# One decoder layer: the sample rows' high and low parts in one stationary tile, 512-wide value and memory products, memory transposes behind task 2, spare transposes in the opening

## The chip, the cores and the metric

The kernel is one program on one core of a Trainium2 chip. The metric is the time of one execution in microseconds of the device, as the median of several runs. TensorE (PE) multiplies: it holds a stationary tile of up to 128 x 128 and streams the columns of a second operand past it, into a bank of PSUM of 512 fp32 columns per partition. VectorE (DVE), ScalarE (ACT) and GpSimd (POOL) do the elementwise work, SyncE (SP) issues the transfers from HBM.

## What is computed

The reference is one inference step of one decoder layer in fp32, for 512 prompt tokens and 64 sample tokens (8 sequences of 8) that share all weights:

```python
h = rmsnorm(x, norm_pre_mix)                       # 1024 channels
ca, cb, hq, hf, hi, hgate, mq, gl = split(h @ w_in)
c     = silu(layernorm(causal_dwconv(ca * sigmoid(cb), conv_w)))   # width 31
p_conv = c @ w_conv_out
o     = hgrn2(silu(hq), hf, v=hi, state)           # 4 heads, chunks of 32
p_hg  = (rmsnorm(o) * silu(hgate)) @ w_hg_out
mk, mv = split(rmsnorm(mem_prompt) @ w_mem_kv)     # 256 memory tokens; sample: cached
p_mem = softmax(mq @ mk.T / sqrt(128)) @ mv @ w_mem_out
g     = sigmoid(gl)                                # three gates of 1024 channels
x     = x + rmsnorm((g0*p_conv + g1*p_hg + g2*p_mem) @ w_out)
x     = x + rmsnorm((silu(h2 @ w_gate) * (h2 @ w_up)) @ w_down)    # h2 = rmsnorm(x)
```

Outputs are both groups' `x`, the last convolution inputs, the recurrent states, and the prompt's memory keys and values.

## The kernel before

**Exactness.** Each fp32 operand of a large product is split into a high part in PE's fast fp32r format and a low part, the remainder (`split`, L99: ACT writes the high part, DVE the low one). A product is three matmuls: high x high, low x high, high x low (`mm3`, L94, and the same written out where the tokens are the stationary operand).

**Tokens.** The 576 tokens form five tiles (`TOK`, L37): four of 128 prompt tokens, and a fifth that begins at token 448, of which only the rows from 64 on, the 64 sample tokens, are used. Where channels are the output rows, tokens are streamed in two groups of 256 and 320 columns (`GRP`, L35). Where tokens are the output rows, a tile of 128 tokens is stationary and the weights are streamed: so in `v_cols` (L688, the recurrence's values), in `mem_kv` (L505, the memory's keys and values, two tiles of 128 memory tokens) and in `mix_out` (L1090, the product with `w_out`). The fifth tile so multiplies 64 prompt rows a second time and throws them away.

**Weights.** `wprep` (L110) loads a chunk of 1024 elements per partition into one of three raw buffers and splits it into one of three pairs of high and low buffers. `wplan` lists the chunks in the order of use, `wahead(n)` keeps n of them prepared (LOOK = 2, L895), `wnext` takes one. For `v_cols` and `mem_kv` a chunk has 512 rows of the weight and 256 columns; a task takes two chunks and does one half of the columns for all its token tiles: four memory tasks and two value tasks.

**Tasks and side work.** The list `tasks` (L1027 to 1057) holds four convolution input tasks (two weight chunks each), four memory tasks, two value tasks, four query tasks, then gates and recurrence heads, and the three branch outputs. Work for the other engines stands in generators that `pump` (L287) advances by a step after, and sometimes inside, each task: `convq` (the 31 taps on DVE, four taps to a step, and the tail), `side` (prompt attention, recurrence) and `sampq` (the sample's attention, `attn_sample`, L590). The order of each engine is then fixed by a scheduler that works from estimated times, with program order as priority; `tc.issue_after(ins)` puts what follows behind an instruction of the same engine.

**The memory rows.** After task 1, `mem_norm` (L494) loads the two tiles of memory tokens, takes their sums of squares on ACT, a reciprocal root on POOL, scales on DVE (L242), transposes on PE in four banks (L250) and splits (L105, L106). It is tied to task 1's last gate on ACT.

**The opening.** Fourteen matmuls of the identity (`WARM`, L184) run while the first tokens load. Then `norm_group` (L236) scales and transposes tiles 0 and 1, and, from `group_b` (L1012), tiles 2 to 4, the sample tile last.

**The sample's memory values.** `attn_sample` loads the cached values in eight units of 512 KB, one unit ahead of the matmuls that use it (L627 to 634).

**Output of the mixer.** `mix_out` takes the tiles in the order 4, 2, 3, 0, 1, each in two halves of 512 columns, 24 matmuls each; `ffn_norm` of a tile follows one tile later, and the feed-forward part begins with the group of tiles 2, 3 and 4. The x pool (`xtile`, L70) has five buffers, which hold the five tiles' residual rows there.

Of the kernel before, what the change touches and what calls it, by code (L numbers as in the profile page):

```python
# [42 lines left out]
def tile_decoder_layer(  # L43
# [17 lines left out]
    seq = [0]  # L61
# [32 lines left out]
    def mm3(out, whi, wlo, xhi, xlo, start, stop, more=False):  # L94
        T.matmul(out, lhsT=whi, rhs=xhi, start=start, stop=False, skip_group_check=more)  # L95
        T.matmul(out, lhsT=whi, rhs=xlo, start=False, stop=False, skip_group_check=more)  # L96
        T.matmul(out, lhsT=wlo, rhs=xhi, start=False, stop=stop, skip_group_check=more)  # L97
# [35 lines left out]
    last = {}  # L133

    def rsqrt(src, n, scale, p0=0, eng=None, eps=None):
# [20 lines left out]
        return y  # L156

# [78 lines left out]
    def norm_group(tiles, g0, hi, lo, c0, n, junk=None, eng=None):  # L236

        for xt, p0 in tiles:  # L240
            r = norm_rows(xt, p0, junk, eng)
            last["scale"] = V.tensor_scalar(xt[p0:, :], xt[p0:, :], r, None, op0=ALU.mult)  # L242
        per, ins = 512 // n, []
        for k0 in range(0, 8, per):
            ps = sdb()
            for kk in range(per):
                o = kk * n
                for xt, p0 in tiles:
                    m = P - p0
                    T.transpose(ps[:, o:o + m], xt[p0:, (k0 + kk) * P:(k0 + kk + 1) * P], ident[p0:, p0:])  # L250
                    o += m
# [4 lines left out]
        return ins  # L256

# [44 lines left out]
    split_a = norm_group([(xts[0], 0), (xts[1], 0)], 0, hhi, hlo, *g0, junk=junk[:, 0:D], eng=A)  # L302
# [191 lines left out]
    def mem_norm():  # L494
        xm = []
        for t in range(2):
            xt = xtile()
            nc.sync.dma_start(xt, mem_prompt[0][P * t:P * t + P, :])
            xm.append((xt, 0))
        mt = big(FR)[:, :4096].rearrange("p (s k t) -> p s k t", s=2, k=8)  # L500
        norm_group(xm, 16, mt[:, 0], mt[:, 1], 0, 256)
# [3 lines left out]
    def mem_kv(s):  # L505
# [7 lines left out]
        dst = mem["k"] if s < 2 else mem["v"]  # L513
        c0 = 256 * (s % 2)
        ws = [wnext(), wnext()]
        mt = mem["mt"]
        for t in range(2):
            ps = mmb()
            for k in range(8):
                hi, lo = ws[k // 4]  # L520
                kk = k % 4
                xh, xl = (mt[:, i, k, P * t:P * t + P] for i in range(2))
                T.matmul(ps[:, :256], lhsT=xh, rhs=hi[:, kk, :], start=k == 0, stop=False)
                T.matmul(ps[:, :256], lhsT=xl, rhs=hi[:, kk, :], start=False, stop=False)
                T.matmul(ps[:, :256], lhsT=xh, rhs=lo[:, kk, :], start=False, stop=k == 7)
            A.activation(dst[:, t, c0:c0 + 256], ps[:, :256], AF.Copy)
        if s == 1:
            nc.sync.dma_start(o_mem_k[0, 0].rearrange("(t p) h d -> p t (h d)", p=P), mem["k"])
        if s == 3:
            nc.sync.dma_start(o_mem_v[0, 0].rearrange("(t p) h d -> p t (h d)", p=P), mem["v"])  # L530
# [59 lines left out]
    def attn_sample():  # L590
# [24 lines left out]
        vc = load(cache_mem_v, 0, 0)  # L615
# [8 lines left out]
        for g in range(2):  # L624
            ops = sdb()
            for j in range(4):
                vj = vc  # L627
                if (g, j) != (1, 3):
                    vc = load(cache_mem_v, *units[4 * g + j + 1])
# [58 lines left out]
    def v_cols(i):  # L688

        values()  # L690
        ws = [wnext(), wnext()]
        for t in range(5):
            c0, p0 = TOK[t]
            ps = mmb()
            for k in range(8):
                hi, lo = ws[k // 4]
                kk = k % 4
                xh, xl = (x[:, k, c0:c0 + P] for x in h)
                T.matmul(ps[:, :256], lhsT=xh, rhs=hi[:, kk, :], start=k == 0, stop=False)  # L699
                T.matmul(ps[:, :256], lhsT=xl, rhs=hi[:, kk, :], start=False, stop=False)  # L700
                T.matmul(ps[:, :256], lhsT=xh, rhs=lo[:, kk, :], start=False, stop=k == 7)  # L701
            A.activation(hg["v"][p0:, t, 256 * i:256 * i + 256], ps[p0:, :256], AF.Copy)
            if t == 2:
                pump(1, 2)

# [199 lines left out]
    def kvspec(s, i):  # L905
        return w_mem_kv[0][512 * i:512 * i + 512, 256 * s:256 * s + 256], 4, 256
# [60 lines left out]
    def kv_task(s):  # L967
        def fn():
            mem_kv(s)
            if s == 3:  # L970
# [13 lines left out]
    def v_task(i):  # L984
        def fn():
            if i == 0:
                hg_consts()
            v_cols(i)
        return fn

    def vspec(i, kh):
        return w_in[0][512 * kh:512 * kh + 512, C_HI + 256 * i:C_HI + 256 * i + 256], 4, 256
# [19 lines left out]
    def group_b():  # L1012
# [5 lines left out]
        return norm_group(xtb, 0, hhi, hlo, *g1, junk=junk[:, D:2 * D], eng=A)  # L1018
# [10 lines left out]
    for s in range(4):  # L1029
        add(kv_task(s), kvspec(s, 0), kvspec(s, 1), conv=2)  # L1030
    for i in range(2):
        add(v_task(i), vspec(i, 0), vspec(i, 1), conv=2, ns=2)
# [28 lines left out]
    for i, (fn, nconv, ns) in enumerate(tasks):  # L1061
# [28 lines left out]
    def mix_out(ti):  # L1090
# [4 lines left out]
        ss = tiny()  # L1095
        for hh in range(2):
            ps = mmb()
            whi, wlo = wo[hh]
            for k in range(8):
                mh, ml = (m[:, k, c0:c0 + P] for m in mhl)  # L1100
# [3 lines left out]
            junk = junk512()  # L1104
            A.activation(junk[p0:, :], ps[p0:, :], AF.Square, accum_out=ss[p0:, hh:hh + 1])
            t = tmp(512)
# [209 lines left out]
    order = (4, 2, 3, 0, 1)  # L1316
# [187 lines left out]
```

## Time and profile before

| | |
|---|---|
| median of 3 runs | 1017.58 us (1017.54 to 1018.92) |
| the profiled execution | 1010.57 us, its span 1008.9 us |
| DMA | 106.58 MB, 106 GB/s over the span |

The profile shows one execution. Its page gives the busy time of each engine, the span in 40 slices, the chain of work that ended last and the costliest groups of instructions. Other views of the same trace are the list of waits, the instructions of one line, the timeline of a stretch with the idle time ahead of an instruction and what ended it in brackets, and the busy time by stretches. PEld are the loads of the stationary tiles, which overlap the matmuls.

### The profile page before, as it was taken

Reading aid. Unit: us, or ns where it says so; the run is one execution under the profiler, and the core shown is the slowest. Engines: PE = TensorE matmul, PEld = TensorE weight load, DVE = VectorE, ACT = ScalarE, POOL = GpSimd, SP = SyncE. Lnnn points to the kernel's source line nnn. Section 1 sums busy time; section 2 is a strip of 40 time slices with the busy share of each in tenths; the row PEclk is TensorE's granted clock in tenths of the full one; section 3 lists DMA queues with packets and bytes.
Section 4 is the critical chain, followed back from the end, with each engine's and each line's share of the span. In section 5 each row is a group of like instructions: output and inputs, shape, how many; then the busy total and the mean of one; then the engine's idle time right before and its main releaser. Section 6 shows DMA issues by size and latency. Waiting matters only on the chain.

```text
span 1008.9 us, 17323 instructions
## 1 busy us (share of the span) xinstructions
PE 991.6 (98%) x7141; PEld 938.6 (93%) x7141; DVE 690.8 (68%) x1232; ACT 433.9 (43%) x769; POOL 34.3 (3%) x127
## 2 busy tenths in 40 slices
PE   7989999999999999999999999999999999999997
PEld 6989999887899999999999889999999999999995
DVE  6689988954775375566549678968877876813805
ACT  6535255574632222213234365444444544614612
POOL 1220000001001001001010000000000000000000
PEclk9999999999999999999999999999999999999999
DMA  8425322533753222222234315023232234321302
GB/s 240 143 79 172 105 84 64 147 92 107 210 157 105 84 84 87 84 87 84 89 103 137 115 50 191 1 85 97 75 122 85 85 124 138 129 86 59 131 16 94
DMA packets 129005, 106.58 MB, mean 106 GB/s; under 512 B 3208, under 2 KB 116388, under 8 KB 128918
## 3 DMA queue, kind: packets, MB, share of 16 engines
q1 hardware_dynamic: 128926, 105.48, 33.9%
q8 instruction: 56, 0.92, 0.4%
q14 instruction: 23, 0.19, 0.1%
HBM read 97.15 MB, written 8.68 MB: 105 GB/s over the span
## 4 chain that ended last, share of the span: by engine, by line
PE 94%; DMA 2%; ACT 1%; DVE 1%; POOL 1%; issue 1%; DVEq 0%; ACTq 0%
PE mm L96 20%; PE mm L97 20%; PE mm L95 20%; PE sd L96 3%; PE sd L95 3%; PE sd L97 3%; PE sd L1414 2%; PE sd L1415 2%; PE sd L1416 2%; PE mm L1101 2%; PE mm L1102 2%; PE mm L1103 2%; PE mm L700 1%; PE mm L699 1%; PE mm L701 1%; PE sd L611 1%
## 5 line engine op out<-in xcount | busy, mean ns | idle before, releaser
L96 PE MATMUL mm<-S,wh 128*128 128x320 f32 (+1 forms) x1216 | 363.5, 299 | 0.3 <-DVE S L106 0.3
L95 PE MATMUL mm<-S,wh 128*128 128x320 f32 (+1 forms) x1216 | 362.1, 300 | 1.0 <-ACT S L105 1.0
L97 PE MATMUL mm<-S,wl 128*128 128x320 f32 (+1 forms) x1216 | 361.9, 299 | 0.0
L97 PEld LDWEIGHTS mm<-S,wl 128*128 128x128 f32 x1216 | 228.4, 188 | 5.0 <-issue 4.2
L95 PEld LDWEIGHTS mm<-S,wh 128*128 128x128 f32 x1216 | 228.1, 188 | 5.1 <-issue 2.3
L96 PEld LDWEIGHTS mm<-S,wh 128*128 128x128 f32 x1216 | 228.6, 188 | 3.3 <-issue 1.1
L103 DVE TENSOR_TENSOR wl<-wr,wh 128x1024 fp32r<-128x1024 f32 x98 | 119.6, 1222 | 122.0 <-ACT wh L102 121.7
L102 ACT ACTIVATE wh<-wr 128x1024 fp32r<-128x1024 f32 x98 | 103.8, 1060 | 211.9 <-PE mm L96 170.4
L394 DVE SCALAR_TENSOR_TENSOR S<-S,cT,S 128x512 f32<-128x512 f32 x120 | 89.9, 749 | 2.7
L96 PE MATMUL mm<-S,wq 128*128 128x288 f32 x216 | 63.7, 295 | 0.0
L97 PE MATMUL mm<-S,wq 128*128 128x288 f32 x216 | 63.7, 295 | 0.0
L96 PE MATMUL sd<-S,wq 128*128 128x288 f32 x216 | 63.6, 295 | 0.0
L95 PE MATMUL sd<-S,wq 128*128 128x288 f32 x216 | 63.6, 294 | 0.0
L95 PE MATMUL mm<-S,wq 128*128 128x288 f32 x216 | 63.6, 294 | 0.0
L97 PE MATMUL sd<-S,wq 128*128 128x288 f32 x216 | 63.1, 294 | 0.0
L102 ACT ACTIVATE wq<-ws 128x1024 fp32r<-128x1024 f32 x36 | 37.9, 1056 | 38.9 <-PE mm L96 31.8
L103 DVE TENSOR_TENSOR wq<-ws,wq 128x1024 fp32r<-128x1024 f32 x36 | 43.8, 1218 | 4.0 <-ACT wq L102 3.9
L103 DVE TENSOR_TENSOR S<-S,S 128x1152 fp32r<-128x1152 f32 (+3 forms) x46 | 44.1, 986 | 1.6 <-ACT S L102 1.6
L96 PEld LDWEIGHTS sd<-S,wq 128*128 128x128 f32 x216 | 40.6, 188 | 0.0
L97 PEld LDWEIGHTS mm<-S,wq 128*128 128x128 f32 x216 | 40.6, 188 | 0.0
L95 PEld LDWEIGHTS sd<-S,wq 128*128 128x128 f32 x216 | 40.5, 188 | 0.0
L96 PEld LDWEIGHTS mm<-S,wq 128*128 128x128 f32 x216 | 40.6, 188 | 0.0
(349 smaller groups left out, 1771.2 us busy)
## 6 DMA issues: line engine op xcount, KB each, us to landing
wr<-in_w_in_dram SPq DMA_DIRECT2D x52, 512.0 KB
wr<-in_w_ffn_down_dram SPq DMA_DIRECT2D x22, 512.0 KB
S<-in_w_ffn_gate_dram SPq DMA_DIRECT2D x9, 1024.0 KB
S<-in_w_ffn_up_dram SPq DMA_DIRECT2D x9, 1024.0 KB
x<-in_x_prompt_dram SPq DMA_DIRECT2D x8, 512.0 KB
wr<-in_w_mem_kv_dram SPq DMA_DIRECT2D x8, 512.0 KB
x<-in_cache_mem_k_dram SPq DMA_DIRECT2D x8, 512.0 KB
x<-in_cache_mem_v_dram SPq DMA_DIRECT2D x8, 512.0 KB
```

Source lines behind the costliest of these rows:

```text
L95: T.matmul(out, lhsT=whi, rhs=xhi, start=start, stop=False, skip_group_check=more)
L96: T.matmul(out, lhsT=whi, rhs=xlo, start=False, stop=False, skip_group_check=more)
L97: T.matmul(out, lhsT=wlo, rhs=xhi, start=False, stop=stop, skip_group_check=more)
L102: A.activation(hi, src, AF.Copy)
L103: (eng or V).tensor_tensor(lo, src, f32(hi), op=ALU.subtract)
L394: queue(V.scalar_tensor_tensor(out=dp, in0=src, scalar=w, in1=dp, op0=ALU.mult, op1=ALU.add))
L1101: T.matmul(ps, lhsT=mh, rhs=whi[:, k, :], start=k == 0, stop=False)
L1102: T.matmul(ps, lhsT=ml, rhs=whi[:, k, :], start=False, stop=False)
L1103: T.matmul(ps, lhsT=mh, rhs=wlo[:, k, :], start=False, stop=k == 7)
L1414: T.matmul(pa[ti], lhsT=ah, rhs=w[0][:, kk, :], start=f == 0, stop=False)
L1415: T.matmul(pa[ti], lhsT=al, rhs=w[0][:, kk, :], start=False, stop=False)
L1416: T.matmul(pa[ti], lhsT=ah, rhs=w[1][:, kk, :], start=False, stop=f == NF - 1)
```

## The change

Six things change.

1. **The sample's rows stacked.** `beside` copies the low and the high parts of the 64 sample tokens next to each other into one x tile: 128 stationary columns for each k, low rows first. `sample_products` then does two matmuls per k instead of three: the stacked tile times the high weights (rows 0 to 63 of PSUM get low x high, rows 64 to 127 high x high), and the 64 high rows times the low weights, added into rows 0 to 63. `sample_sum` copies rows 0 to 63 with ACT to the partitions from 64 on and adds rows 64 to 127 to them with DVE. Used for the fifth tile in `v_cols` and in `mix_out`, where the square and the gain then read the sum.
2. **512 columns.** `v_cols` and `mem_kv` do all 512 columns at once and take the weights in four chunks of 256 rows by 512 columns, the loop over chunks outside and over token tiles inside. One value task and two memory tasks remain. `v_cols` holds five PSUM banks throughout (four of the mm tag, one of the sd tag); `wahead` is called for each chunk; the steps of the side generators are pumped inside the loop (two convolution steps in each memory task, and in the value task one convolution and two side steps at chunks 0 and 2).
3. **The memory transposes later.** `norm_group` is cut into `norm_scale` and `norm_turn`; `mem_norm` yields between them. The first part stays where it was, the second is tied to the last matmul of task 2.
4. **Spare transposes.** In the opening, `fill` transposes the identity into the bank ahead of the last tile's transposes: six in the first group, eight in the second.
5. **Cached values two ahead.** `attn_sample` issues two loads of the cached values where it issued one, and keeps two ahead.
6. **The order of `mix_out`** becomes 2, 4, 3, 0, 1.

```diff
+    def beside(act):
+        x = px.tile([P, 8, P], FR, tag="x", name=nm("hs"))
+        for i, part in enumerate((act[1], act[0])):
+            A.activation(x[:, :, 64 * i:64 * i + 64], f32(part)[:, :, SEQ:NT], AF.Copy)
+        return x
+
+    def sample_products(ps, act, stack, k, whi, wlo):
+        if k == 0:
+            T.matmul(ps, lhsT=stack[:, k, :], rhs=whi, start=True, stop=False)
+        T.matmul(ps[:64, :], lhsT=act[0][:, k, SEQ:NT], rhs=wlo, start=False, stop=False)
+        if k:
+            T.matmul(ps, lhsT=stack[:, k, :], rhs=whi, start=False, stop=k == 7)
+
+    def sample_sum(dst, ps):
+        A.activation(dst[64:, :], ps[:64, :], AF.Copy)
+        V.tensor_tensor(dst[64:, :], ps[64:, :], dst[64:, :], op=ALU.add)
...
+    def fill(out, n):
+        for _ in range(n):
+            T.transpose(out, ident, ident)
...
+                    if fills and i == len(tiles) - 1:
+                        fill(ps[:, o:o + P], fills)
+                        fills = 0
...
         dst = mem["v" if s else "k"]
+        pss = [mmb(), mmb()]
+        for i in range(4):
+            hi, lo = wnext()
+            wahead(LOOK)
+            for t in range(2):
+                ps = pss[t]
+                for kk in range(2):
+                    k = 2 * i + kk
+                    xh, xl = (mt[:, z, k, P * t:P * t + P] for z in range(2))
+                    T.matmul(ps, lhsT=xh, rhs=hi[:, kk, :], start=k == 0, stop=False)
+                    T.matmul(ps, lhsT=xl, rhs=hi[:, kk, :], start=False, stop=False)
+                    T.matmul(ps, lhsT=xh, rhs=lo[:, kk, :], start=False, stop=k == 7)
+            if i == 1:
+                pump(2)
...
-        vc = load(cache_mem_v, 0, 0)
+        vcs = deque(load(cache_mem_v, *units[u]) for u in range(2))
...
+        hs = beside(h)
+        pss = [mmb() for _ in range(4)] + [sdb()]
+        for i in range(4):
+            hi, lo = wnext()
+            wahead(LOOK)
+            for t in range(5):
+                for kk in range(2):
+                    k = 2 * i + kk
+                    if t == 4:
+                        sample_products(pss[t], h, hs, k, hi[:, kk, :], lo[:, kk, :])
+                        continue
...
+            if i in (0, 2):
                 pump(1, 2)
...
         if i == 1:
-            side.append(mem_norm())
+            memory = mem_norm()
             with tc.issue_after(gated[-1].ins):
+                next(memory)
+        if i == 2:
+            with tc.issue_after(last["mm"].ins):
+                side.append(memory)
                 drain(side)
...
-    order = (4, 2, 3, 0, 1)
+    order = (2, 4, 3, 0, 1)
```

More of the change, by code (lines that the diff above doesn't have):

```diff
@@ L59, in tile_decoder_layer @@
     pd = ctx.enter_context(tc.tile_pool(name="pd", bufs=5, space=bass.MemoryType.DRAM))
-    seq = [0]
+    seq, last = [0], {}
     def nm(s):
@@ L96, in mm3 @@
         T.matmul(out, lhsT=whi, rhs=xlo, start=False, stop=False, skip_group_check=more)
-        T.matmul(out, lhsT=wlo, rhs=xhi, start=False, stop=stop, skip_group_check=more)
+        last["mm"] = T.matmul(out, lhsT=wlo, rhs=xhi, start=False, stop=stop, skip_group_check=more)
     def split(hi, lo, src, scale=None, eng=None):
@@ L247, in norm_group @@
                 o = kk * n
-                for xt, p0 in tiles:
+                for i, (xt, p0) in enumerate(tiles):
                     m = P - p0
+                    if fills and i == len(tiles) - 1:
+                        fill(ps[:, o:o + P], fills)
+                        fills = 0
                     T.transpose(ps[:, o:o + m], xt[p0:, (k0 + kk) * P:(k0 + kk + 1) * P], ident[p0:, p0:])
@@ L256, in norm_group @@
         return ins
+    def norm_group(tiles, *args, junk=None, eng=None, fills=0):
+        norm_scale(tiles, junk, eng)
+        return norm_turn(tiles, *args, fills)
     def wcols(w, c, n=P):
@@ L512, in mem_kv @@
             mem["q"] = kv[:, 2048:4096].rearrange("p (j t) -> p j t", j=4)
-        dst = mem["k"] if s < 2 else mem["v"]
-        c0 = 256 * (s % 2)
-        ws = [wnext(), wnext()]
+        dst = mem["v" if s else "k"]
         mt = mem["mt"]
-        for t in range(2):
[L518 to L530, printed above, removed]
+        pss = [mmb(), mmb()]
[12 more added lines that the diff above has]
+                pump(2)
+        for t in range(2):
+            A.activation(dst[:, t, :], pss[t], AF.Copy)
+        out = (o_mem_v if s else o_mem_k)[0, 0]
+        nc.sync.dma_start(out.rearrange("(t p) h d -> p t (h d)", p=P), dst)
     def mem_kT():
@@ L626, in attn_sample @@
             for j in range(4):
-                vj = vc
-                if (g, j) != (1, 3):
-                    vc = load(cache_mem_v, *units[4 * g + j + 1])
+                vj, u = vcs.popleft(), 4 * g + j + 2
+                if u < 8:
+                    vcs.append(load(cache_mem_v, *units[u]))
                 for mh in range(2):
@@ L686, in values, with v_cols @@
             hg["v"] = hg["vv"][:, :2560].rearrange("p (t c) -> p t c", t=5)
-    def v_cols(i):
+    def v_cols():
         values()
[L691 to L703, printed above, removed]
+        hs = beside(h)
[9 more added lines that the diff above has]
+                        continue
+                    xh, xl = (x[:, k, P * t:P * t + P] for x in h)
+                    T.matmul(pss[t], lhsT=xh, rhs=hi[:, kk, :], start=k == 0, stop=False)
+                    T.matmul(pss[t], lhsT=xl, rhs=hi[:, kk, :], start=False, stop=False)
+                    T.matmul(pss[t], lhsT=xh, rhs=lo[:, kk, :], start=False, stop=k == 7)
+            if i in (0, 2):
                 pump(1, 2)
+        for t in range(4):
+            A.activation(hg["v"][:, t, :], pss[t], AF.Copy)
+        sample_sum(hg["v"][:, 4, :], pss[4])
     def hg_alloc(j):
@@ L1028, in tile_decoder_layer @@
         add(conv_task(j), win(C_CB + P * j), win(C_CA + P * j), conv=1)
[L1029 to L1032, printed above, removed]
+    for s in range(2):
+        add(kv_task(s), *(kvspec(s, i) for i in range(4)), conv=2)
+    add(v_task, *(vspec(i) for i in range(4)), conv=2, ns=2)
     for j in range(4):
```

38 lines of the change are left out of this document (22 added, 16 removed).

## The prediction

> **What bounds the kernel now.** I read the page first, then the list of waits, then the timeline at each place that the change touches.
>
> ```profile
> span 1008.9 us, 17323 instructions
> PE 991.6 (98%) x7141; PEld 938.6 (93%) x7141; DVE 690.8 (68%) x1232; ACT 433.9 (43%) x769; POOL 34.3 (3%) x127
> PEclk9999999999999999999999999999999999999999
> ```
>
> PE (TensorE's matmuls) is busy for 98% of the span, at the full granted clock; PEld, its weight loads, overlaps it, and no other engine passes 68%. So a matmul taken away shortens the run by its spacing, and a PE wait taken away shortens it by its length. The list of PE's waits is short (seven rows, of which these five are the longest; us in total, times, longest):
>
> ```profile
> PE sd L250 <- DVE tn L215: 2.7, 1, 2.7
> PE sd L250 <- DVE x L242: 2.0, 2, 1.0
> PE sd L185 <- POOL ident masks.py:199: 1.8, 1, 1.8
> PE sd L633 <- DMA x<-in_cache_mem_v_dram: 1.7, 2, 1.2
> PE mm L95 <- ACT S L105: 1.0, 3, 0.4
> ```
>
> The first is the memory transposes, the second and the last are the opening, the fourth is the sample group's memory values. The change aims at both kinds: fewer PE cycles, and three of these waits.
>
> **Price of a matmul.** A row's duration contains the latency of the pipeline; what counts is the distance between starts. For 256 columns I take the value product, whose 240 matmuls (80 on each of three lines) run without a gap; for 512 columns a stretch of `mix_out` whose first and last rows stand here, 86 matmuls in an unbroken series.
>
> ```profile
> L699 PE MATMUL mm<-wh,S x80: 279/281/285, 99.9 to 128.0; 128*128 128x256 f32 x80
> L701 PE MATMUL mm<-wl,S x80: 279/281/285, 100.2 to 128.3; 128*128 128x256 f32 x80
> ```
> ```profile
> 563.18 0.39 PE L1101 MATMUL mm<-S,S 128*128 128x512 f32 x1
> ...
> 582.45 0.39 PE L1102 MATMUL mm<-S,S 128*128 128x512 f32 x1
> ```
>
> 256 columns: (128.3 - 99.9)/239 = 118.8 ns. 512 columns: (582.45 - 563.18)/85 = 226.7 ns. Two narrow ones are 237.6 ns, so a pair that becomes one wide matmul saves 10.9 ns, not half.
>
> [...]
>
> **The three products.**
> - Memory keys and values: 192 matmuls of 256 columns (4 x 2 x 24) become 96 of 512. 192 x 118.8 = 22.81 us, 96 x 226.7 = 21.76 us: 1.05 us less.
> - Value columns: 240 of 256 columns become 4 tiles x 24 of 512, and for the sample tile two per k: 16. 240 x 118.8 = 28.51 us, 112 x 226.7 = 25.39 us: 3.12 us less. Of the sample's two matmuls per k, one has only 64 stationary columns. It streams the same 512 columns, so I price it like the others; no row has this form, and its other bound is half that price, which for the 24 narrow ones of the whole change would be another 2.7 us.
> - `mix_out` for the sample tile: 48 become 32, 16 x 226.7 = 3.63 us less.
>
> Together 7.80 us of PE time, with no wait in any of the three places before that could hide it.
>
> **What these products add on other engines.** The weights now come in chunks of two k by 512 columns, the same 1024 elements per partition. A kv chunk lasts 12 x 226.7 = 2.72 us, a value chunk 28 x 226.7 = 6.3 us. The turn-over of one chunk, from PE's release of the buffer to the finished low half, is shown by an ACT row and a DVE row of this stage:
>
> ```profile
> 85.12 1.06 ACT L102 ACTIVATE wh<-wr 128x1024 fp32r<-128x1024 f32 x1 [1.71 <-PE mm L524]
> ```
> ```profile
> 87.24 1.22 DVE L103 TENSOR_TENSOR wl<-wr,wh 128x1024 fp32r<-128x1024 f32 x1
> ```
>
> 87.24 + 1.22 - 85.12 = 3.3 us. With three buffers the next two chunks cover 5.4 us. ACT waits here for PE, not for a DMA, so the raw data lie ready. I take no cost.
>
> The stacked tile costs two ACT copies of 512 elements, and the sum of the two halves one ACT copy and one DVE addition of 64 x 512. The nearest rows:
>
> ```profile
> L539 ACT ACTIVATE S<-sd 128x512 f32<-128x512 f32 x2 | 1.1, 596 | 0.0
> ```
> ```profile
> L1107 DVE TENSOR_TENSOR tb<-mm,gB 64x512 f32<-64x512 f32 x2 | 1.4, 695 | 1.2 <-ACT jk L1105 1.2
> ```
>
> That is about 1.2 us before and 1.3 us behind the products. In the value product, tile 4 comes after 24 other matmuls (5.4 us), and its sum is used much later: hidden. In `mix_out` the copies need all eight blocks of the merged activations, whose last low half is this row:
>
> ```profile
> 556.66 0.48 DVE L103 TENSOR_TENSOR S<-S,S 128x320 fp32r<-128x320 f32 x1
> ```
>
> It ends at 557.1; two copies later is 558.4. On PE `mix_out` runs from 548.2:
>
> ```profile
> L1101 PE MATMUL mm<-S,S x80: 389/389/504, 548.2 to 603.7; 128*128 128x512 f32 x80
> ```
>
> Tile 2, now first, takes 48 x 226.7 = 10.9 us, to 559.1. The cover is 0.7 us, and tile 3 is there to be pulled ahead. I take nothing; if ACT holds the copies back it costs up to the 3.6 us of a rival below. The sixth x buffer that `mix_out` now wants comes free with tile 4's products, some 25 us before the last tile needs it.
>
> In the value product five PSUM banks are held through the whole of it, four of the mm tag and one of the sd tag. Tile 0 is finished 22 matmuls (5 us) before the end, its eviction is under a microsecond, and the next task wants one bank at first: no wait. The key transposes that now fall into this stretch need one sd bank at a time, and three are left.
>
> **The memory transposes.**
>
> ```profile
> 52.45 0.63 PE L250 MATMUL sd<-ident,x 128*128 128x128 f32 x4
> ...
> 54.23 0.28 PE L97 MATMUL mm<-S,wl 128*128 128x256 f32 x1
> 57.21 1.53 PE L250 MATMUL sd<-ident,x 128*128 128x128 f32 x12 [2.70 <-DVE tn L215]
> ...
> 63.52 0.28 PE L95 MATMUL mm<-S,wh 128*128 128x256 f32 x1
> ```
> ```profile
> 55.76 1.39 DVE L242 TENSOR_SCALAR x<-x,tn 128x1024 f32<-128x1024 f32 x1 [1.99 <-POOL tn L155]
> ...
> 64.15 1.25 DVE L106 SCALAR_TENSOR_TENSOR S<-sd,gT,S 128x256 fp32r<-128x256 f32 x3
> ```
>
> PE came to the second tile's transposes in the middle of task 2's input products and stood for 2.70 us until DVE had scaled the tile (55.76 + 1.39 = 57.15). Loads, statistics and scale keep their place; only the 16 transposes and their splits go behind the last matmul of task 2. That task ended at 63.52, where the next begins; without the wait and without the transposes inside it (0.63 + 1.53 us) it ends near 58.7, 1.5 us after the scale. So the wait goes whole: 2.70 us. The transposes themselves are paid as before. Their splits ended at 65.4 before, 8.2 us behind the start at 57.21. Now they have task 3 in front of the first memory product, which came at 76.3, 12.8 us after 63.52. SP sees no other order: the two loads are issued where they were.
>
> ```profile
> L523 PE MATMUL mm<-wh,S x64: 274/281/367, 76.3 to 99.6; 128*128 128x256 f32 x64
> ```
>
> **The sample's memory values.**
>
> ```profile
> 249.70 0.45 SPq L594 DMA_DIRECT2D x<-in_cache_mem_v_dram  x1
> 258.81 12.37 SPq L594 DMA_DIRECT2D x<-in_cache_mem_v_dram  x7
> ```
> ```profile
> 265.28 0.64 PE L633 MATMUL sd<-x,x 128*32 128x128 f32 x16 [0.56 <-DMA x<-in_cache_mem_v_dram]
> 267.09 0.64 PE L633 MATMUL sd<-x,x 128*32 128x128 f32 x16 [1.16 <-DMA x<-in_cache_mem_v_dram]
> ```
>
> One load goes out at 249.70, the other seven in a burst from 258.81, and PE waits for units 1 and 2, 0.56 + 1.16 = 1.72 us. With two loads at the earlier place, unit 1 is there, and unit 2 takes the burst's first slot, landing by 265.3 instead of 267.1. I take the 1.72 us as gone; the bound is none of it, if no buffer is free at 250.
>
> **The opening.**
>
> ```profile
> 1.81 6.06 PE L185 MATMUL sd<-ident 128*128 128x128 f32 x28 [1.81 <-POOL ident masks.py:199]
> ...
> 9.55 1.53 PE L250 MATMUL sd<-ident,x 128*128 128x128 f32 x12 [1.03 <-DVE x L242]
> ...
> 18.36 1.32 PE L250 MATMUL sd<-ident,x 128*128 128x128 f32 x8
> 20.64 0.46 PE L250 MATMUL sd<-ident,x 64*128 64x64 f32 x4 [0.96 <-DVE x L242]
> ```
>
> Twelve transposes in 1.53 us, less the 0.27 of a single one (the median below), are 115 ns each.
>
> ```profile
> L250 PE MATMUL sd<-ident,x x56: 222/273/328, 8.0 to 58.5; 128*128 128x128 f32 x48, 64*128 64x64 f32 x8
> ```
>
> Six spare ones (0.69 us) fit into the 1.03 us before 9.55, eight (0.92 us) into the 0.96 us before 20.64, and what ends both waits is DVE. Cost zero; uncovered, 1.6 us. Is there a gain? The warm-up ran at 6.06/28 = 216 ns a record, and after the 1.03 us of idling the transposes and all that follows ran at full pace. In this execution the gap cost nothing but itself, and I take zero.
>
> **The sum.** 7.80 + 2.70 + 1.72 = 12.2 us. The profiled execution took 1010.57 us (span 1008.9): it would take 998.4. The runs shown have a median 7.0 us above it, for a reason that the trace doesn't show; I carry the difference over: 1017.6 - 12.2 = 1005.4 us. The case's own range is 1002.7 (narrow sample matmuls at half price) to 1007.0 (spare transposes uncovered). About 0.2%, 2 us, is what a measurement can tell from no change.
>
> **Rivals.**
>
> *Only the products pay.* The order of each engine is fixed before the run from estimates, and the old transposes show that they can be wrong by 2.7 us at this spot. If the scale or the loads again come late by as much, 7.8 us remain: 1009.8. For it: the margin is 1.5 us. Against it: the issue point is now tied to a matmul, not to an estimate.
>
> *The stack is late in `mix_out`.* The copies stand in ACT's order among weight splits that wait for DMAs, as here, and PE stands at tile 4:
>
> ```profile
> 554.42 1.06 ACT L102 ACTIVATE S<-wr 128x1024 fp32r<-128x1024 f32 x1 [5.29 <-DMA wr<-in_w_out_dram]
> ```
>
> The saving of 3.63 us is eaten: 1009.0. Against it: tile 3's products can go first.
>
> *The opening's clock.* In other executions the idle stretches of the opening may drop the clock back to the warm-up's half pace, and the spare transposes prevent it. If one input product of the opening, 24 matmuls of 118.8 ns, runs at half pace, it takes 2.9 us more; the gain would be 15.1 us: 1002.5. The rows above, where nothing falls back, speak against it. [...]
>
> *Slower: the weights of the kv product become the bound.* DVE is full here:
>
> ```profile
> 85.00:90.00 5.00, 5.00 (x44) 5.00 (x43) 4.96 (x6) 2.78 (x4) 0.00 (x0) 1.00 0.58 174
> ```
> ```profile
> L394 DVE SCALAR_TENSOR_TENSOR S<-S,cT,S 128x512 f32<-128x512 f32 x120 | 89.9, 749 | 2.7
> ```
>
> The new code queues two convolution steps in the middle of each memory task and two behind it, 8 taps x 0.749 = 6.0 us at a time. Standing ahead of a low half, such a block makes the turn-over 9.3 us against 5.4 us of cover, and PE stands 3.9 us. Four such blocks in the two tasks are 15.6 us, 3.4 us more than the gain: 1021.0. It decides from the fourth block on; three leave no measurable change. Against it: before, DVE was as full, and PE waited for no low half in this stage.
>
> **How the numbers follow.** Forecast 0.58, only the products 0.17, late stack 0.10, clock 0.06, kv weights 0.09 (0.05 slower, 0.04 no change). Faster 0.91, same 0.04, slower 0.05. The predicted time is 1005.4. The range takes in the clock case, the late stack and the case of the products alone, 1001.5 to 1010.5, and leaves out the kv case and the thin ends.
>
> **What would show it.** Right: 96, 112 and 224 matmuls of 512 columns in the three products, 227 ns apart; no PE wait of microseconds at the memory transposes and at L633's successor; waits in the opening gone as waits but with the same starts behind them; PE's busy time down by about 8 us. Wrong: a PE wait for ACT or DVE on a weight tile between 70 and 125 us, one at the sample tile of `mix_out`, an opening that is longer or shorter by over 1 us, or matmuls of 512 columns at another spacing.

## The result and the profile after

The changed kernel takes 1004.64 us (median of 4 runs, 1004.50 to 1005.55), the kernel before 1017.56 us beside it (4 runs, 1015.62 to 1018.92): ratio 0.9876, 95% interval 0.9859 to 0.9893, 12.9 us less where 12.2 were forecast. The total is right. In the traces its parts are not: the two profiled executions lie only 5.1 us apart (spans 1008.9 and 1003.8). The timed runs of the kernel before stand 5 to 8 us above its own profile, and those of the changed kernel stand on theirs. Where those 7 us come from is the main question of the experiments.

The page of the changed kernel, the lines that answer to the first ones of before:

```profile
span 1003.8 us, 16880 instructions
PE 986.9 (98%) x6915; PEld 924.0 (92%) x6915; DVE 693.3 (69%) x1235; ACT 433.5 (43%) x766; POOL 33.5 (3%) x127
```

PE is still the bound, 4.7 us less busy (991.6 before), where the prediction looked for about 8. Its list of waits down to 0.4 us (us in total, times, longest):

```profile
PE sd L204 <- POOL ident masks.py:199: 1.8, 1, 1.8
PE sd L671 <- DMA x<-in_cache_mem_v_dram: 1.5, 2, 1.0
PE sd L489 <- DVE tb L487: 1.2, 1, 1.2
PE mm L95 <- ACT S L105: 1.0, 3, 0.4
PE sd L280 <- DVE x L259: 0.8, 1, 0.8
PE sd L1179 <- ACT tb L1176: 0.8, 1, 0.8
PE sd L671 <- ACT x L660: 0.7, 1, 0.7
PE mm L95 <- DVE S L771: 0.5, 1, 0.5
PE mm L562 <- DVE wl L103: 0.4, 1, 0.4
```

The 2.7 us at the memory transposes are gone. The wait for the sample group's memory values is there as before (1.5 us, 1.7 before), and five waits that the list of before does not have stand beside it: for the convolution's normalization (at L489), for ACT (its instructions at L660 and L1176), for a DVE product of the recurrence (L771) and for the low half of a kv weight (at L562). The edited places, in order of time:

```profile
7.90 0.82 PE L264 MATMUL sd<-ident 128*128 128x128 f32 x6
...
9.77 1.64 PE L280 MATMUL sd<-ident,x 128*128 128x128 f32 x13 [0.83 <-DVE x L259]
...
19.41 1.04 PE L264 MATMUL sd<-ident 128*128 128x128 f32 x8
20.28 1.03 PE L280 MATMUL sd<-ident,x 128*128 128x128 f32 x7
...
59.04 1.91 PE L280 MATMUL sd<-ident,x 128*128 128x128 f32 x16
```
```profile
L560 PE MATMUL mm<-wh,S x32: 390/392/404, 73.5 to 96.6; 128*128 128x512 f32 x32
L562 PE MATMUL mm<-wl,S x32: 390/394/500, 74.0 to 97.0; 128*128 128x512 f32 x32
L741 PE MATMUL mm<-wh,S x32: 390/393/477, 97.3 to 121.7; 128*128 128x512 f32 x32
L170 PE MATMUL sd<-wh,hs x7: 392/392/395, 100.8 to 123.1; 128*128 128x512 f32 x7
L1149 PE MATMUL mm<-S,S x64: 389/389/476, 545.6 to 597.9; 128*128 128x512 f32 x64
L1151 PE MATMUL mm<-S,S x64: 388/389/504, 546.0 to 598.4; 128*128 128x512 f32 x64
```

In the kernel before, the last matmuls of the kv product and of `mix_out`:

```profile
L525 PE MATMUL mm<-wl,S x64: 278/281/363, 76.5 to 99.8; 128*128 128x256 f32 x64
L1103 PE MATMUL mm<-S,S x80: 387/389/396, 548.7 to 604.2; 128*128 128x512 f32 x80
```

Against before: the kv product starts 2.8 us earlier (73.5 for 76.3) and takes as long (first to last start 23.5 us in both). The value product, from its first matmul to the next stage's, takes 26.1 us instead of 28.5: 2.4 less. From there to `mix_out` 2.4 us are lost again (from 128.4 to 548.2 before, from 123.35 to 545.6 now). `mix_out` is 3.2 us shorter (first to last start 52.8 for 56.0), and 0.8 of that goes into the new wait at L1179, behind it. That is 2.8 + 2.4 - 2.4 + 3.2 - 0.8 = 5.2 us, the difference of the spans within its rounding. Where the 2.4 us go, the timeline shows at the sample group's memory values:

```profile
257.28 0.85 PE L489 MATMUL sd<-tb,ones 128*128 128x128 f32 x4 [1.17 <-DVE tb L487]
258.24 0.83 PE L658 MATMUL sd<-ident,x 128*128 128x128 f32 x4
259.76 2.79 PE L671 MATMUL sd<-x,x 128*32 128x128 f32 x48 [0.69 <-ACT x L660]
263.06 0.64 PE L671 MATMUL sd<-x,x 128*32 128x128 f32 x16 [0.51 <-DMA x<-in_cache_mem_v_dram]
264.17 0.39 PE L95 MATMUL mm<-S,wh 128*128 128x256 f32 x1 [0.47 <-DVE S L771]
...
273.11 0.65 PE L671 MATMUL sd<-x,x 128*32 128x128 f32 x16 [0.98 <-DMA x<-in_cache_mem_v_dram]
```

PE comes here some 5 us earlier than before and waits for everything that has not become earlier with it. And the 48 small matmuls take 2.79 us, where 16 of the same shape take 0.64. The granted clock says why (columns: stretch; length and then busy time with instructions of PE, PEld, DVE, ACT, POOL; granted clock; DMA share; GB/s):

```profile
256.00:259.50 3.50, 1.79 (x9) 0.99 (x8) 2.19 (x5) 2.97 (x8) 0.00 (x0) 1.00 0.11 32
259.50:262.90 3.40, 2.79 (x48) 2.18 (x48) 3.37 (x10) 3.37 (x5) 0.00 (x0) 0.50 0.73 220
```

PE was idle for half of 3.5 us, and then the clock was granted at half pace for 3.4 us. The traces here also end with such a stretch, behind PE's last matmul, where it costs PE nothing: in this profile it begins at 1000.2 us, 3.7 us behind that matmul, in the profile of before 2.6 us behind it. The profiled execution of before has that last one alone (from 1004.1 us on), and its mean clock of 0.998 comes from it.

### The profile page after: what moved, and what is told of

Read it like the earlier page. It is cut to its first block, busy times and chain, and to the rows that moved or that the text cites. A ratio compares the mean times of both kernels' runs of the same rounds, so it can differ in the third digit from the quotient of the medians.

```text
span 1003.8 us, 16880 instructions
## 1 busy us (share of the span) xinstructions
PE 986.9 (98%) x6915; PEld 924.0 (92%) x6915; DVE 693.3 (69%) x1235; ACT 433.5 (43%) x766; POOL 33.5 (3%) x127
## 4 chain that ended last, share of the span: by engine, by line
PE 82%; DVE 7%; DMA 5%; ACT 2%; issue 2%; POOL 1%; SPq 0%; DVEq 0%; ACTq 0%
PE mm L96 18%; PE mm L95 18%; PE mm L97 18%; PE sd L96 3%; PE sd L95 3%; PE sd L97 3%; PE sd L1465 2%; PE sd L1466 2%; PE sd L1467 2%; DVE wl L103 1%; DMA x<-in_cache_mem_v_dram 1%; DMA wr<-in_w_ffn_gate_dram 1%; DVE S L428 1%; DMA wr<-in_w_out_dram 1%; DVE S L106 1%
## 5 line engine op out<-in xcount | busy, mean ns | idle before, releaser
L102 ACT ACTIVATE S<-S 128x1152 fp32r<-128x1152 f32 (+3 forms) x46 | 38.1, 864 | 6.9 <-DVE S L521 4.9
L97 PEld LDWEIGHTS mm<-S,wq 128*128 128x128 f32 x216 | 40.6, 188 | 0.0
```

The costliest lines, as they stand in the source:

```text
L97: last["mm"] = T.matmul(out, lhsT=wlo, rhs=xhi, start=False, stop=stop, skip_group_check=more)
L102: A.activation(hi, src, AF.Copy)
```

## The experiments

Theory A: the opening's clock. Theory B: the wait at the memory transposes. Theory C: the distance between profile and runs belongs to no part. All ratios below are to the kernel before on the same chip; e1 to e4, c0, f1, p1 and c1 ran on one chip, g3, b2 and k1 on a second, h1 on a third.

**e1, the spare transposes alone.**

```diff
-                for xt, p0 in tiles:
+                for i, (xt, p0) in enumerate(tiles):
                     m = P - p0
+                    if fills and i == len(tiles) - 1:
+                        fill(ps[:, o:o + P], fills)
+                        fills = 0
...
-    split_a = norm_group([(xts[0], 0), (xts[1], 0)], 0, hhi, hlo, *g0, junk=junk[:, 0:D], eng=A)
+    split_a = norm_group([(xts[0], 0), (xts[1], 0)], 0, hhi, hlo, *g0, junk=junk[:, 0:D], eng=A, fills=6)
...
-        return norm_group(xtb, 0, hhi, hlo, *g1, junk=junk[:, D:2 * D], eng=A)
+        return norm_group(xtb, 0, hhi, hlo, *g1, junk=junk[:, D:2 * D], eng=A, fills=8)
```

> The kernel before with the fourteen spare transposes and nothing else. The changed kernel gained 12.9 us in the timed runs but only 5.1 us between the two profiled executions (span 1008.9 to 1003.8), since the timed runs of the kernel before lie about 7 us above its own profile and those of the changed kernel do not. Theory A, the opening's clock: the spare transposes keep the clock in executions where it would drop; then this kernel loses the 7 us and comes out near 1010.5, with a trace like the kernel before. Theory B, the wait at the memory transposes is what is longer in those executions: this kernel stays at 1015.6 to 1018.9. Theory C, the distance to the profile is a matter of the execution and belongs to neither part: also no change, 1015.6 to 1018.9, and the distance shows up in other kernels too.

Measured: 1015.96 us beside 1015.46, ratio 1.0004 (0.9987 to 1.0021). The spare transposes alone bring nothing. But this profile is of a long execution (span 1015.9, mean clock 0.993), and shows what the short one of before did not. The memory transposes:

```profile
57.65 2.61 PE L258 MATMUL sd<-ident,x 128*128 128x128 f32 x11 [2.86 <-DVE x L247]
```
```profile
54.00:56.90 2.90, 0.79 (x7) 0.58 (x5) 0.89 (x2) 2.44 (x3) 2.32 (x9) 1.00 0.01 3
56.90:63.70 6.80, 6.05 (x28) 6.06 (x29) 6.80 (x16) 3.55 (x8) 0.14 (x1) 0.50 0.24 77
```

PE waits there as before (2.86 us, 2.70 before), and then the clock is at half pace for 6.8 us. The same stretch of the kernel before, in its profile:

```profile
54.00:57.20 3.20, 0.51 (x5) 0.31 (x3) 1.44 (x3) 2.02 (x3) 2.11 (x8) 1.00 0.01 3
57.20:64.00 6.80, 6.79 (x53) 6.79 (x54) 6.80 (x16) 3.73 (x9) 0.00 (x0) 1.00 0.24 80
```

53 PE instructions there, 28 here: the same wait costs its length in one execution and some 3 us more in another. So the profile of before was of an execution without any such loss. Its 31 runs on this chip show the same dependence: the 8 with a mean clock of 0.996 or 0.997 have a median of 1013.7 us, the 9 with 0.990 or 0.991 one of 1019.3, and a line through all 31 (span against span times one minus clock, correlation 0.92) reaches full clock at 1009.0 us. But time at half pace is not the whole distance. The median run of the 31 lies 4.9 us above the profile, which was not taken among them. Its mean clock of 0.995 means 5.1 us lost, (1 - 0.995) x 1013.7, where a stretch at half pace counts with half its length; the profile has 2.4 us by the same count, half of the 4.7 of its last stretch. So some 3 of the 4.9 us are time at half pace, by this estimate. The rest stays open, and so do the 2 us by which the result's runs lie higher still, whose clocks are not on record.

**e2, the changed kernel without its spare transposes.**

```diff
-    split_a = norm_group([(xts[0], 0), (xts[1], 0)], 0, hhi, hlo, *g0, junk=junk[:, 0:D], eng=A, fills=6)
+    split_a = norm_group([(xts[0], 0), (xts[1], 0)], 0, hhi, hlo, *g0, junk=junk[:, 0:D], eng=A)
...
-        return norm_group(xtb, 0, hhi, hlo, *g1, junk=junk[:, D:2 * D], eng=A, fills=8)
+        return norm_group(xtb, 0, hhi, hlo, *g1, junk=junk[:, D:2 * D], eng=A)
```

> The changed kernel without its fourteen spare transposes. Theory A: the 7 us come back, 1010 to 1012, and the timed runs scatter by 1 us or more as those of the kernel before did (1015.6 to 1018.9). Theory B and theory C: 1004.4 to 1004.8, since the starts behind the two waits in the opening were the same with and without the spare ones (10.94 against 11.16, 21.53 against 21.74).

Measured: 1009.47 us (1006.08 to 1011.57), ratio 0.9941 (0.9920 to 0.9962), clock down to 0.990. Beside c0 below it is 4.3 us slower. Theory A holds in the changed kernel with 4.3 of its 7 us, where it failed in the kernel before; the profile has the clock at half pace from 22.8 to 29.6 us. It has it a second time, for 10.2 us from 261.7 on, at the sample group's memory values, where the changed kernel's own profile has 3.4 us; so not all of the 4.3 us need be lost in the opening.

**e3, the later memory transposes alone.**

```diff
-            side.append(mem_norm())
+            memory = mem_norm()
             with tc.issue_after(gated[-1].ins):
-                drain(side)
+                next(memory)
+        if i == 2:
+            with tc.issue_after(last["mm"].ins):
+                side.append(memory)
+                drain(side)
```

> The kernel before with the memory transposes behind the last matmul of task 2 and nothing else. Theory B: the wait of 2.7 us goes and with it the 7 us that the profile does not show: 1007 to 1008. Theories A and C: the wait alone goes, 2.7 us: 1014.9.

Measured: 1012.14 us (1008.88 to 1014.26), ratio 0.9958 (0.9939 to 0.9977): 3.3 us, between the theories and with the wait's own 2.7 us inside the interval. Theory B in its full size is out. This profile has no loss at the memory transposes, but a long one in the opening, which has no spare transposes here:

```profile
20.89 0.46 PE L260 MATMUL sd<-ident,x 64*128 64x64 f32 x4 [0.96 <-DVE x L239]
```
```profile
19.00:22.30 3.30, 1.82 (x12) 1.04 (x10) 3.10 (x8) 1.76 (x4) 0.00 (x0) 0.99 0.82 229
22.30:32.50 10.20, 9.94 (x35) 7.97 (x35) 3.83 (x8) 3.79 (x7) 0.00 (x0) 0.50 0.54 150
```

**e4, the changed kernel with the early memory transposes.**

```diff
                 next(memory)
-        if i == 2:
-            with tc.issue_after(last["mm"].ins):
                 side.append(memory)
                 drain(side)
```

> The changed kernel with the memory transposes issued where the kernel before had them, in the middle of task 2. Theory B: the wait comes back with the 7 us: 1014 to 1015. Theories A and C: 1007.3, the wait of 2.7 us alone.

Measured: 1010.51 us (1008.77 to 1013.07), ratio 0.9947 (0.9931 to 0.9963), 5.4 us above c0: the wait of 2.86 us that is back in its profile, and a stretch at half pace behind it (58.1 to 61.5 us). Another stretch of 3.4 us, from 607.7 on, stands behind a wait of 1.70 us for ACT after `mix_out`; c0's profile has none there. So in the changed kernel the later transposes are worth about twice their wait.

**c0, the changed kernel once more, beside its variants.**

> The changed kernel itself once more, beside the variants on one chip. What the four variants showed: the granted clock falls to half pace for stretches of about 3.3, 6.8 or 10 us at three places, each behind idle PE time: the second group of the opening, the memory transposes, and the sample group's memory values. Theory A+B, both the spare transposes and the later memory transposes take one such place away: this kernel is left with the third, mean clock 0.996 to 0.997, 1004 to 1006, where the kernel before has 1012.6 to 1020.6. Theory C, the steadiness is that of the chip used last: 1005 to 1011 here, with a clock down to 0.990.

Measured: 1005.16 us (1004.08 to 1005.95) beside 1015.92, ratio 0.9891 (0.9865 to 0.9917), clock 0.996 to 0.997 in every run. Here the whole change is worth 10.8 us, where the result has 12.9. Theory C is out. In the opening:

```profile
18.60:22.30 3.70, 3.15 (x24) 2.31 (x22) 3.50 (x8) 2.15 (x4) 0.00 (x0) 1.00 0.68 177
22.30:32.50 10.20, 9.93 (x62) 8.46 (x62) 4.49 (x10) 4.46 (x8) 0.00 (x0) 1.00 0.56 145
```

With the eight spare transposes PE is busy for 3.15 of the 3.70 us ahead of 22.3, and full clock follows: 62 instructions in the stretch in which e3 got through 35.

**h1, the changed kernel with the second eight spare transposes only.**

```diff
-    split_a = norm_group([(xts[0], 0), (xts[1], 0)], 0, hhi, hlo, *g0, junk=junk[:, 0:D], eng=A, fills=6)
+    split_a = norm_group([(xts[0], 0), (xts[1], 0)], 0, hhi, hlo, *g0, junk=junk[:, 0:D], eng=A)
```

> The changed kernel without the first six spare transposes, the eight of the second group kept. In the two profiles in which the clock fell in the opening it fell at 22.6 to 22.9 us, right behind the second group's waits, and never behind the 1.5 us of idling of the first group (8.2 to 9.7 us). If only the second place counts: as the changed kernel, 1004 to 1006, mean clock 0.996 to 0.997, no stretch at half pace before 200 us. If the first six count as well: part of the 4.3 us of the run without any comes back, 1006.5 to 1009.5, clock down to 0.991 in some executions.

Measured: 1005.31 us (1003.79 to 1005.69), ratio 0.9893 (0.9870 to 0.9916), and its profile has no loss before 258 us; the clock is 0.996 or 0.997 in five runs of six and 0.992 in the other. The eight do it; the six can go, though PE idles 1.5 us where they were:

```profile
PE sd L280 <- DVE x L259: 1.5, 1, 1.5
```

**f1, 28 more spare transposes at the sample group's memory values.**

```diff
+            if t == 3:
+                fill(pr[1][:, P:2 * P], 10)
             dg = tmp(P)
...
+                nf = {(0, 0): 6, (0, 3): 4, (1, 3): 8}.get((g, j), 0)
+                with tc.issue_after(tx.ins):
+                    fill(ops[:, P * j:P * j + P], nf)
```

> The changed kernel with 28 more spare transposes at the sample group's memory values: ten among the diagonal products of the convolution's normalization, six and four ahead of the first and fourth unit of the first group, eight ahead of the last unit of the second. If idle PE time is what lowers the clock there, the clock stays at 1.00 between 255 and 275 us, the mean clock is 0.998 or 0.999 and the time is 2 to 3 us below the changed kernel: 1001.5 to 1003. If the drop has another cause (the small matmuls with 32 stationary columns themselves), the clock falls there all the same and the spare ones cost up to 28 x 0.115 = 3.2 us: 1004.6 to 1008.

Measured: 1011.69 us (1009.25 to 1013.54), ratio 0.9950 (0.9931 to 0.9968): 6.5 us slower than c0, and neither theory's number. The order of the DMA issues had moved. SP's queue in c0, then in f1:

```profile
246.81 12.61 SPq L632 DMA_DIRECT2D x<-in_cache_mem_v_dram  x4
259.51 0.53 SPq L112 DMA_DIRECT2D wr<-in_w_conv_out_dram  x1
260.81 5.82 SPq L632 DMA_DIRECT2D x<-in_cache_mem_v_dram  x4
```
```profile
246.45 2.02 SPq L634 DMA_DIRECT2D x<-in_cache_mem_v_dram  x2
258.65 0.37 SPq L112 DMA_DIRECT2D wr<-in_w_conv_out_dram  x1
259.11 9.90 SPq L634 DMA_DIRECT2D x<-in_cache_mem_v_dram  x6
```

The planner put a convolution weight, which waits for its buffer until 258.65, ahead of the third value load, and PE stood 3.49 us for that load. The clock then fell:

```profile
260.60:263.40 2.80, 0.07 (x4) 0.00 (x0) 2.22 (x7) 2.07 (x3) 0.00 (x0) 1.00 1.11 334
263.40:270.20 6.80, 5.83 (x48) 4.60 (x49) 6.80 (x14) 4.62 (x10) 0.00 (x0) 0.50 1.14 294
```

**g3, 14 of them, placed so that SP's order stays.** Against f1:

```diff
-            if t == 3:
-                fill(pr[1][:, P:2 * P], 10)
+            if t == 4:
+                fill(pr[1][:, P:2 * P], 8)
...
-                nf = {(0, 0): 6, (0, 3): 4, (1, 3): 8}.get((g, j), 0)
+                nf = {(0, 0): 6}.get((g, j), 0)
```

> The changed kernel with 14 more spare transposes at the sample group's memory values, eight among the diagonal products and six ahead of the first unit, chosen so that SP keeps the order of the changed kernel (four value loads ahead of a convolution weight). The run with 28 had that order changed, two loads ahead of the weight, and PE waited 3.5 us for the third. If idle PE time lowers the clock: it stays at 1.00 from 255 to 265 us, mean clock 0.999 and 1002 to 1003. If the small matmuls themselves lower it: it falls there as in the changed kernel, 1005 to 1006.

Measured: 1006.33 us (1004.68 to 1008.45), ratio 0.9904 (0.9880 to 0.9928): no gain over c0 (0.9891). The clock stayed at 1.00 up to 264 us, as it should if idle time is the cause, and four of six runs had 0.998 or 0.999; even the best of them took 1004.68. PE came to the loads earlier and waited for them instead, and in the profiled execution the clock fell behind that:

```profile
263.04 0.64 PE L676 MATMUL sd<-x,x 128*32 128x128 f32 x16 [1.49 <-DMA x<-in_cache_mem_v_dram]
264.92 0.58 PE L95 MATMUL mm<-S,wh 128*128 128x256 f32 x1 [1.24 <-DVE S L776]
```
```profile
255.00:264.00 9.00, 6.40 (x95) 5.04 (x94) 5.95 (x15) 7.69 (x13) 0.00 (x0) 1.00 0.57 176
264.00:270.80 6.80, 5.88 (x27) 5.88 (x28) 5.42 (x12) 4.13 (x11) 0.00 (x0) 0.50 1.11 287
```

In this stage the loads and the convolution's tail set the pace, and PE's clock is not what holds it.

**p1, the products alone.** The kernel before with the three products and `mix_out`'s order from the change; the edit is that of e2, e4 and c1 made together in the changed kernel.

> The kernel before with the three products as in the changed kernel, and nothing of the other parts: early memory transposes, no spare ones, one value load ahead. By the forecast's terms the products are worth 7.8 us: 1007.7 beside 1015.5 of the kernel before. From the trace of the changed kernel they are worth less, 0 + 2.4 + 3.2 = 5.6 us: 1009.9, with the clock falling as often as before (mean 0.990 to 0.996).

Measured: 1012.62 us (1009.37 to 1015.84), ratio 0.9972 (0.9953 to 0.9991), clock 0.988 to 0.997: 3.3 us, less than either number. Its PE comes earlier to the same waits and is slowed behind them more often: 2.73 us at the memory transposes with a stretch at half pace behind it, 2.9 us for a DVE operation that is queued behind the convolution's tail (L771), and another stretch at 270.

**b2, spare transposes and later memory transposes, without the products.** The edit is that of e1 and e3 together in the kernel before.

> The kernel before with the spare transposes and the later memory transposes, without the products. Alone the spare ones brought nothing (1015.96 beside 1015.46) and the later transposes 3.3 us (1012.14). If the two add up: 1012 to 1012.5. If the opening's clock was kept only for the memory wait to lose it again, then they are worth more together: 4.3 us more than the later transposes alone, as the changed kernel without spare ones showed (1009.47 beside 1005.16): 1008 to 1009, clock 0.997 or more, and the products are then worth only 3 to 4 us of the changed kernel's gain; with the forecast's 7.8 us for the products it has to stand near 1013.

Measured: 1012.95 us (1011.81 to 1015.39) beside 1016.25, ratio 0.9973 (0.9959 to 0.9987). They are not worth more together than the later transposes alone: the clock holds in the opening and at the memory transposes, and in the profiled execution it falls at 267 us, behind waits of 1.1 and 1.1 us for the value loads and 0.8 us for that DVE operation. This kernel and c1 differ by the products alone (with `mix_out`'s order): 1012.95 to 1006.04, 6.9 us, though on two chips (7.7 by the two ratios, give or take 2.8). Where the clock is held in the opening and at the memory transposes, the products are worth what the forecast gave them, 7.8, within the scatter; in p1, where it is not, 3.3.

**c1, the changed kernel with one value load ahead.**

```diff
-        vcs = deque(load(cache_mem_v, *units[u]) for u in range(2))
+        vc = load(cache_mem_v, 0, 0)
...
-                vj, u = vcs.popleft(), 4 * g + j + 2
-                if u < 8:
-                    vcs.append(load(cache_mem_v, *units[u]))
+                vj = vc
+                if (g, j) != (1, 3):
+                    vc = load(cache_mem_v, *units[4 * g + j + 1])
```

> The changed kernel with one value load ahead, as the kernel before had it. By the forecast's term the second load ahead is worth 1.72 us: 1006.4. By the trace of the changed kernel, where 0.51 + 0.98 us of waiting for these loads were left and 0.69 us for ACT stood ahead of them, it is worth nothing: 1004.4 to 1005.0.

Measured: 1006.04 us (1004.19 to 1006.78), ratio 0.9897 (0.9874 to 0.9921) where c0 has 0.9891: nothing that can be told from zero. SP's queue is the same in its trace, four value loads, the convolution weight, four value loads.

**k1, the changed kernel with the kv product in 256 columns.**

```diff
-        return w_mem_kv[0][256 * i:256 * i + 256, 512 * s:512 * s + 512], 2, 512
+        return w_mem_kv[0][512 * i:512 * i + 512, 256 * s:256 * s + 256], 4, 256
...
-    for s in range(2):
-        add(kv_task(s), *(kvspec(s, i) for i in range(4)), conv=2)
+    for s in range(4):
+        add(kv_task(s), kvspec(s, 0), kvspec(s, 1), conv=2)
```

> The changed kernel with the keys and values of the memory in 256 columns, as the kernel before had them. By the forecast's term it is 1.05 us slower, 1006.2 beside 1005.2, with the stage from the first to the last kv matmul at 24.8 us; by the trace, where the wide stage took 23.75 us and the narrow one 23.65, it is the same within 0.3 us and the stage takes 23.6 to 23.7.

Measured: 1009.20 us (1008.08 to 1011.50), ratio 0.9936 (0.9914 to 0.9958). The stage takes 24.7 us from first to last start, 1.2 more than the wide one in the same place:

```profile
L559 PE MATMUL mm<-wh,S x64: 278/282/369, 73.4 to 97.9; 128*128 128x256 f32 x64
L561 PE MATMUL mm<-wl,S x64: 274/281/388, 73.7 to 98.1; 128*128 128x256 f32 x64
```
```profile
PE mm L561 <- DVE wl L103: 0.8, 1, 0.8
```

0.8 us of it is a wait for a low half that the narrow kernel of before, 2.9 us later in the run, did not have. The timed difference to c0 is larger than that; this version also has another order of value loads on SP and 2.9 us of waiting for that DVE operation, so its time doesn't isolate the kv product.

## Why the prediction was right in its total

- **The carried difference was the largest error.** "For a reason that the trace doesn't show; I carry the difference over": the 7 us were not carried over, for the runs of the changed kernel stand on their profile. Against this stand about 7 us of the 12.2 that the traces do not show (5.1 between the profiles). That the two errors cancel is luck. Part of the difference was time at half pace, by the estimate under e1 some 3 us in a median run of before, while its profile has none that costs PE time. The mean clock of before goes from 0.989 to 0.999 over its runs, that of the changed kernel (c0) stays within 0.996 to 0.997. But the profile of before is also a rarely short execution: its 1010.57 us are below all 79 runs of that kernel beside the experiments (the shortest 1011.27). At one clock, 0.996 or 0.997, the kernels are some 8.5 us apart (1013.7 under e1, 1005.16 for c0), more than the profiles say.
- **The parts in the timed runs.** Spare and later transposes together 3.3 us (b2), the products 6.9 (b2 to c1), the second load 0.9 (c1 to c0, not to be told from zero): 11.1 us, beside the 10.8 of c0. The terms of the forecast for them were 2.70, 7.80 and 1.72. So the runs bear out the two large terms within the scatter; the traces give less for the products, and why is not shown.
- **The clock rival was no rival but part of the result.** It put the opening's stretch at 2.9 us for one product at half pace and gave it a chance of 0.06. Leaving the spare transposes out costs 4.3 us (e2 against c0), and at the memory transposes the clock falls as well (6.8 us at half pace in e1, 3.4 us in e4), which no line of the prediction had. "In this execution the gap cost nothing but itself" was true of that execution only; a gap that costs nothing in one execution was taken as one that costs nothing. The warm-up, whose 216 ns a record the rival took for half pace, has a granted clock of 1.00 in the trace (1.81 to 7.80 us); half pace, 0.50, stands in the openings of e2 and e3. The stretches last 3.4, 6.8 and 10.2 us, as one, two and three steps of 3.41 us would (the longest, in e3, from 22.23 to 32.47 us). So do the starts fit: within one execution they lie whole multiples of 3.413 us apart (259.52 and 1000.21 in the profile of the changed kernel, 217 of 3.4133 us; 58.24 and 269.84 in p1, 62; 22.77 and 261.70 in e2, 70). The step is an estimate from these lengths and starts; what sets it is not shown.
- **Memory transposes: right.** The 2.70 us went as worked out: they start at 59.04 without a wait, the kv product 2.8 us earlier. In the timed runs they are worth more, 3.3 us (e3) and 5.4 (e4 against c0).
- **512 columns: the price was of another stage.** 226.7 ns is the spacing in `mix_out`. In the value product, 48 matmuls in an unbroken series:

```profile
110.13 0.39 PE L170 MATMUL sd<-wh,hs 128*128 128x512 f32 x1
...
121.05 0.40 PE L741 MATMUL mm<-wh,S 128*128 128x512 f32 x1
```

  (121.05 - 110.13)/47 = 232.3 ns. Against 118.8 a pair saves 5.3 ns, not 10.9: kv 0.5 us instead of 1.05, the value columns 2.5 instead of 3.12 (28.51 - 112 x 0.2323; measured 2.4). For the three products together the traces have 5.6 us (0, 2.4 and 3.2), where the forecast has 7.80. Another spacing than 227 ns was one of the prediction's own signs of being wrong. The upper choice for 64 stationary columns was right, they cost as much as 128: one of them starts at 115.94 us (L168) and the next matmul at 116.17, 0.23 us later.
- **kv: the low half came late, but once.** The kv rival's mechanism, also a sign of being wrong, showed as one wait of 0.40 us, not as four of 3.9, and with the spacing it left nothing of the term in the profile.
- **`mix_out`: right.** 3.2 of 3.63 us; no wait stands inside it, so the stack was not late, but ACT was 0.81 us late behind it (L1179).
- **The value loads: wrong.** "I take the 1.72 us as gone": 1.49 us are left, and c1 shows no gain from the edit that can be told from zero. SP issues four loads ahead of the convolution weight, which waits for its buffer, and four behind it, with one or with two ahead in the code; p1 with one ahead has the same order, so it was the other edits that changed the one and seven of before. The second failure there is that PE, 5 us early, meets ACT, DVE and the loads, which are not earlier: 2.4 us of the gain is given back in this stage.

Why a stretch begins in one execution and not in another at the same wait (2.70 us without in the profile of before, 2.73 us with in p1's), the traces show in part. If the steps of 3.413 us run on through the whole execution (the author's estimate, carried on from the starts of the stretches), they lie differently in each. In p1 nearly the whole wait lies in one step (54.83 to 58.24, PE busy 0.87 us); in before a boundary at 55.22, 278 steps ahead of the last stretch at 1004.1, cuts it, with 2.70 and 1.42 us busy in the two. The idle time of the opening lies in one step in e2 and e3 (1.75 and 1.93 us busy), where the clock fell, and is cut in before and p1 (2.38 and 2.41), where it did not. But busy time alone does not decide: 1.42 us had no drop behind it, 2.14 us in h1 (255.23 to 258.65) had one. What else counts stays open, and no run here could set the phase. No version tried beats the changed kernel; h1 equals it with six transposes fewer.

## What to carry to other kernels

One profile is one execution: where the runs lie some us above it and scatter, compare the mean granted clock of the runs before explaining anything, and look in the trace for PE idle times like those behind which the clock fell here, 0.96 us (the opening of e3) to 3.49 us (f1). A wait of PE can then be worth more than its length (2.86 us of waiting and 5.4 us of time, e4 against c0), and a few spare matmuls inside it may pay (eight were worth about 4 us here: e2 without any is 4.3 us above c0, h1 with the eight alone equals it) as long as the stage behind it is bound by PE; where loads set the pace, they were worth nothing (ratio 0.9904 in g3, 0.9891 in c0). Of the time saved ahead of that stage 2.4 us were given back in it, so price each part on a kernel that has the others.

## What the runs showed of the hardware

- The granted clock has two values in these traces, 1.00 and 0.50. All 18 stretches at half pace in the 14 profiles, the last one of each aside, last 3.4 us (11), 6.8 us (5) or 10.2 us (2), and in one execution their starts lie whole multiples of 3.413 us apart (62 in p1, 70 in e2, and 217 to the last one in the profile of the changed kernel).
- In the 3.41 us ahead of each of them PE was busy for 0.7 us (f1) to 2.1 us (h1), so it was never idle throughout. A time as idle as that is not always followed by one (1.42 us busy from 55.22 to 58.63 in the profile of before, and a granted clock of 1.00 up to 1004.1).
- With eight spare transposes in the opening's second group none of ten profiles has a loss there; of the four without, two have (e2 from 22.8 to 29.6 us, e3 from 22.2 to 32.5).
- A 512-column matmul starts every 227 ns in `mix_out` and every 232 ns in the value product (the series from 563.18 us in the kernel before, from 110.13 us in the changed one); no run separates the reason.
